# Narrow decay products, scaled rows and reordered last products in a one-core hybrid decoder step

## The chip, the cores and the metric

The kernel runs on one core of one Trainium2 chip. The metric is the device time of one execution in microseconds; the time of a version is the median of its runs.

## What is computed

One layer of a hybrid decoder, for 256 prompt rows and 8 sample rows (264 columns, since activations are held transposed, channels on the partitions), with a model width of 2048. All of it is in fp32. Cut to what matters:

```python
mod = silu(c) @ w_ada + b_ada                      # 6 vectors of 2048 per row
h   = rmsnorm(x) * (1 + sc1) + sh1
z   = h @ w_in                                     # 2048 -> 15376
y_a = spatial gating (LayerNorm, causal 128x128 per group)
y_b = HGRN2 recurrence, 8 heads of 128x128
y_c = GLA recurrence, 4 heads of 128x256
merged = sum_n sigmoid(z_gate_n) * (y_n @ w_branch[n])
x  = x + gt1 * rmsnorm(merged @ w_out)
h2 = rmsnorm(x) * (1 + sc2) + sh2
x  = x + gt2 * rmsnorm(square(relu(h2 @ w_up)) @ w_down)      # 2048 -> 8192 -> 2048
```

The two recurrences are S_t = diag(f_t) S_(t-1) + k_t v_t^T, o_t = S_t^T q_t. Inside a chunk they need, for positions s before t, the products att[t, s] = sum_d q[t, d] k[s, d] exp(b[t, d] - b[s, d]), where b is the running sum of the log decays. The kernel splits them by distance into levels: at level m, two neighbouring blocks of m positions share a reference point, so the decay factors fall apart into one for k and one for q, and one matrix product gives the block.

## The kernel before

**Dense products.** Every weight is read once, in blocks of 512 KB. ScalarE casts each half block to an fp32r high part (`whi`), VectorE subtracts to get the low part (`wlo`); this is `split_half`, with `split` at line 108. TensorE multiplies high by high, high by low and low by high: lines 641, 642, 643. Twenty-four such products are a *granule* (line 631), and the kernel has 578 of them. A granule's weights are split two to three granules ahead of use (`ahead`, line 613): after granule i, the split of granule i+3 is emitted.

**Order.** The order on TensorE and GpSimd is written out by hand in the mixer part, that on TensorE, VectorE and ScalarE around the begin of the MLP (lines 1481 to 1640), and that on TensorE alone in the rest; where it is not, a scheduler decides. After each granule `background` (line 681) runs a piece of other work. It advances a clock `now` by one and pumps two queues of generators, `bg` (the mixers) and `bs` (the states of the samples), at rates set by `RATES` (line 37).

**Mixers.** `mixer_r` (line 1103) runs three times, for two groups of four HGRN2 heads and one of four GLA heads. The levels for distances 16, 8, 4, 2, 1 and the diagonal are put into the list `levels`. `slot` (line 648) takes up to two of them between two granules and multiplies each as 32 products of 32 columns by 32, in the four 32-column quarters of the array (line 661); `copy_predicated` merges the result (line 1136). Levels 32 and 64 each have 8 products with 128 stationary and 64 moving columns (line 1190), of which the parts needed are copied to `att`; they run at a place of their own. After them come the products over distance 128 (line 1214), transposes (line 1221) and the states. `slot` also takes the sample products (line 668) and the `ada` products for `mod` (line 362).

**Begin of the MLP.** The input of the MLP must be the normed rows, transposed. `quad(q)` (line 1543) makes four of the 16 channel tiles. `quad(0)` adds the residual within TensorE. For q > 0, `residual(q)` (line 1536, VectorE) first adds it in place, and `quad` multiplies each 128x128 piece of the rows by `diag(r2)` (line 1560), which scales and transposes in one. `put_quad` (line 1569) modulates, splits and stores. In `begin_up` (line 1588) the quads and residuals stand between the first eight granules: quad 1 after granule 0, residual 2 after granule 1, quad 2 after granule 2, and so on; the tiles of quad q are first read by granule 2q.

**End.** In the last pass of `down` (line 1622) each of eight blocks of 256 channels is gated, and its rows are transposed back (`to_tokens`, line 828, four transposes) after the next granule. After the last block, three of the eight 128x512 output pieces are made on TensorE: identity times residual (line 1666), then diag(r3) times the rows (line 1675). `norms` (line 1445) has the products that give the last norm, `r3`.

Of the kernel before, what the change touches and what calls it, by code (L numbers as in the profile page):

```python
# [15 lines left out]
P = 128  # L16
# [19 lines left out]
CHUNKS = (2, 2, 4, 4, 4)  # L36
RATES = ((1.8, 0.5), (1.6, 0.5), (1.25, 0.5), (1.0, 0.5))
ST_BUFS = 4
# [19 lines left out]
def hybrid_step_kernel(  # L58
# [396 lines left out]
    hh, hl = [], []  # L455
    A1 = const([P, KT, NC], "A1")
# [115 lines left out]
    class Stream:  # L572
# [27 lines left out]

        def split_half(self, i):
# [3 lines left out]
            split(self.raw[i].pop(0), hi, lo)  # L605
            self.parts.setdefault(i, []).append((hi, lo))

        def split(self, i):
# [39 lines left out]
    def slot():  # L648

        lv = [x for x in levels if x[0] + AGE <= now[0]][:2]  # L650
        sv = [x for x in samples if x[0] + AGE <= now[0]]
        del levels[:len(lv)]
        del samples[:len(sv)]
        if lv:
            pl = sm([P, 2, 8, 32])
            for i, (_, lhs, rhs, _) in enumerate(lv):
                for h in range(4):
                    for hf in range(2):
                        for b in range(4):
                            t0 = hf * P + b * 32  # L660
                            T.matmul(pl[32 * b:32 * b + 32, i, 2 * h + hf, :], lhs[:, h, t0:t0 + 32], rhs[:, h, t0:t0 + 32], start=True, stop=True)  # L661
        if sv:
# [6 lines left out]
        if rounds.due():  # L669
            rounds.steps()  # L670
        for i, (_, _, _, put) in enumerate(lv):
            put(pl[:, i])
        if sv:
# [105 lines left out]
    rows = first.rows()  # L779
    stream[0].split_half(0)  # L780
    next(rows)
# [321 lines left out]
    def mixer_r(G):  # L1103
# [30 lines left out]
        def level(li, lhs, rhs):  # L1134
            def put(ps):
                V.copy_predicated(a32, msk[:, li:li + 1, :].to_broadcast([P, 8, 32]), ps)

            levels.append((now[0], lhs, rhs, put))

        level(5, k, q)  # L1140
        for li, m in enumerate(LEVELS):
# [19 lines left out]
            yield  # L1161
        yield lambda: not levels
        for b in range(4):
            r = slice(32 * b, 32 * b + 32)
            S.copy(att[r, :, r], a32[r])
        yield

        for m in (32, 64):
            n = NP // (2 * m)
            e = blk()  # L1170
            ev, cv = v4(e, 2 * m), v4(c, 2 * m)
# [11 lines left out]

            yield READY
            ps = sm([P, 8, 64])
            for h in range(4):
                for hf in range(2):
                    b = e[:, h, P * hf:P * hf + P]
                    rhs = b.rearrange("p (n j) -> p n j", j=2 * m)[:, :, m:2 * m]
                    T.matmul(ps[:, 2 * h + hf, :].rearrange("p (n j) -> p n j", j=m), b, rhs, start=True, stop=True)  # L1190
            yield
            if m == 32:
                S.copy(att[0:32, :, 32:64], ps[0:32, :, 0:32])
                S.copy(att[64:96, :, 96:128], ps[64:96, :, 32:64])
            else:
                S.copy(att[0:64, :, 64:128], ps[0:64])
# [18 lines left out]
        yield  # L1215
        S.copy(attx, ps)
        kt = blk([P, 2, 512])
        for hf in range(2):
# [323 lines left out]

    def quad(q):

# [3 lines left out]
        for i2 in range(2):  # L1548
# [3 lines left out]
            for i in range(2):  # L1552
# [5 lines left out]
                for t in range(2):  # L1558
                    o = pk[:, t * P:(t + 1) * P]
                    T.matmul(o, x1[t][q // 2][:, c0:c0 + P], dg[:, t, :], start=True, stop=q > 0)  # L1560
                    if q == 0:
                        T.matmul(o, og[t][0][:, c0:c0 + P], dg[:, 2 + t, :], start=False, stop=True)
# [17 lines left out]
    quad(0)  # L1580
    residual(1)

    rate[:] = (0.0, 0.0)
# [4 lines left out]
    def begin_up():  # L1588

        accs = [new_acc(), new_acc()]  # L1590
        for k in range(0, KT, 2):
            granule(w_mlp_up[0], 0, 2, 0, 2 * CW, accs, h2H, h2L, k, k == 0, k + 2 == KT)
            if k % 4 == 0 and k + 4 < KT:
                quad(k // 4 + 1)
            elif k + 6 < KT:
                residual(k // 4 + 2)
            elif k + 2 == KT:
                residual(0)
            if k >= 8:
                background()  # L1600
# [18 lines left out]
    y2 = [blk() for _ in range(4)]  # L1619
    yt = None  # L1620

    def down(f, ah, al):
        for m in range(8):
# [9 lines left out]
            if f == NFB - 1:  # L1633
                g = gated(m, dst, G2)
                if m < 7:
                    later.append((now[0], lambda m=m, g=g: put_rows(m, to_tokens(g), yt)))
                else:
                    return g

    zs = begin_up()  # L1640
# [21 lines left out]

    pt = to_tokens(g)
    for i, p in enumerate(by_pe):
        sums_pe[p] = acc[:, i, :] if i < 2 else sm()
        T.matmul(sums_pe[p], ident, piece(x1, *p), start=True, stop=False, skip_group_check=True)
        if i == 1:
            r3 = norms()
    put_rows(7, pt, yt)
# [73 lines left out]
```

## Time and profile before

| | us |
|---|---|
| Median of 3 runs | 1939.91 (1939.54 to 1941.91) |
| The profiled execution | 1938.26 |
| its span, first to last instruction | 1936.5 |
| VectorE busy | 1186.6 (61%) |
| ScalarE busy | 1002.7 (52%) |

The profile is of one execution. Its groups list, per source line, the busy time, the mean duration of one instruction in ns, and the idle time of the engine just before. Matmuls overlap in the records: a row of 0.28 us doesn't mean that the next one starts 0.28 us later, so distances between starts are used below. An fp32 product shows as two records, an fp32 transpose and an fp32r product as one.

### The profile page before, as it was taken

The page shows a single profiled execution, that of the slowest core. Times are in us where ns is not written, and L with a number is a line of the kernel's source. Part 1 is how long each engine was busy: PE and PEld are TensorE (multiplying, and loading weights), DVE is VectorE, ACT ScalarE, POOL GpSimd, SP SyncE. Part 2 cuts the span into 40 slices and gives each one's busy share as a digit, 9 for nine tenths or more (in the row PEclk, how much of TensorE's full clock was granted, in tenths as well). Part 3 has the DMA queues.
Part 4 walks back from the last instruction along what each step waited for, and adds up shares of the span by engine and source line. Part 5 has one row for each costly group of instructions (what it writes and reads, how often), then busy time and mean ns, then how long its engine had stood idle before and what let it go on. Part 6 is the DMA issues. An engine that isn't in the chain of part 4 may idle for free.

```text
span 1936.5 us, 42145 instructions
## 1 busy us (share of the span) xinstructions
PE 1903.5 (98%) x17012; PEld 1813.5 (94%) x17012; DVE 1186.6 (61%) x2092; ACT 1002.7 (52%) x1818; POOL 84.8 (4%) x146
## 2 busy tenths in 40 slices
PE   7999999999999999999999999999999999999998
PEld 5889999999999989899999989999999999999997
DVE  4566667686676784555555666545556555555665
ACT  5434454665855755544444555444444545454544
POOL 1000000001101111100000010000000000000000
PEclk9999999999999999999999999999999999999999
DMA  9897786778778778887777846676665656555552
GB/s 334 318 331 252 232 299 205 227 257 263 230 254 253 228 255 262 288 271 250 255 257 230 302 124 214 221 239 185 184 181 179 185 177 184 180 180 182 180 182 100
DMA packets 339395, 442.05 MB, mean 228 GB/s; under 512 B 14946, under 2 KB 281040, under 8 KB 339200
## 3 DMA queue, kind: packets, MB, share of 16 engines
q1 hardware_dynamic: 329136, 409.62, 65.8%
q0 software_dynamic: 8992, 28.48, 4.5%
q8 instruction: 133, 2.18, 0.4%
q10 hardware_dynamic: 1072, 1.25, 0.2%
q14 instruction: 62, 0.51, 0.1%
HBM read 427.60 MB, written 11.70 MB: 227 GB/s over the span
## 4 chain that ended last, share of the span: by engine, by line
PE 95%; DMA 3%; DVE 1%; ACT 1%; issue 0%; SPq 0%; POOL 0%; DVEq 0%; ACTq 0%
PE mm L641 29%; PE mm L642 28%; PE mm L643 28%; PE ada L362 3%; DMA b<-in_w_ada_dram 2%; PE ada L294 1%; DMA vbc<-vs_d 1%; PE sm L833 1%; PE sm L661 1%; PE sm L1190 1%; PE sm L668 1%; DMA b<-in_x_prompt_dram 0%; PE sm L1560 0%; DMA raw<-in_w_in_dram 0%; DVE wlo L106 0%
## 5 line engine op out<-in xcount | busy, mean ns | idle before, releaser
L641 PE MATMUL mm<-b,whi 128*128 128x264 f32 x4624 | 1325.2, 287 | 2.4 <-ACT b L109 1.6
L643 PE MATMUL mm<-b,wlo 128*128 128x264 f32 x4624 | 1311.9, 284 | 4.1 <-DVE wlo L106 2.6
L642 PE MATMUL mm<-b,whi 128*128 128x264 f32 x4624 | 1313.0, 284 | 1.9 <-issue 1.0
L106 DVE TENSOR_TENSOR wlo<-raw,whi 128x512 fp32r<-128x512 f32 x1136 | 776.7, 689 | 561.8 <-ACT whi L109 557.9
L109 ACT CAST whi<-raw 128x512 fp32r<-128x512 f32 x1136 | 696.1, 618 | 741.7 <-PE mm L642 654.8
L641 PEld LDWEIGHTS mm<-b,whi 128*128 128x128 f32 x4624 | 869.8, 188 | 44.7 <-issue 26.7
L643 PEld LDWEIGHTS mm<-b,wlo 128*128 128x128 f32 x4624 | 869.4, 188 | 6.2 <-DVE wlo L106 3.4
L642 PEld LDWEIGHTS mm<-b,whi 128*128 128x128 f32 x4624 | 869.7, 188 | 1.5 <-DVE b L106 1.2
L103 DVE TENSOR_TENSOR b<-b,mm 128x528 f32<-128x528 f32 (+1 forms) x137 | 95.7, 699 | 41.9 <-PE mm L643 41.7
L1087 DVE SCALAR_TENSOR_TENSOR st<-vbc,b,st 128x128 f32<-128x128 f32 (+1 forms) x96 | 34.2, 390 | 59.6 <-DMA vbc<-vs_d 56.2
L1085 ACT ACTIVATE st<-st,fs 128x128 f32<-128x128 f32 (+1 forms) x96 | 37.2, 431 | 53.9 <-DMA st<-in_state_hgrn_dram 27.2
L362 PE MATMUL ada<-araw,cT 128*32 128x512 f32 x296 | 39.8, 601 | 0.0
L294 PE MATMUL ada<-b,cT 128*32 128x256 f32 (+1 forms) x640 | 35.0, 353 | 3.2 <-DMA b<-in_w_ada_dram 3.0
L100 DVE TENSOR_TENSOR b<-b,b 128x512 f32<-128x512 f32 (+1 forms) x47 | 33.8, 740 | 1.3 <-ACT b L1203 1.1
L294 PEld LDWEIGHTS ada<-b,cT 128*32 128x32 f32 x640 | 17.8, 113 | 15.8 <-DMA b<-in_w_ada_dram 7.6
L1088 POOL DMA_DIRECT2D out_dram<-st x32 | 23.5, 735 | 127.7 <-DVE st L1087 122.9
L362 PE MATMUL ada<-b,cT 128*32 128x512 f32 x216 | 26.2, 593 | 0.0
L106 DVE TENSOR_TENSOR b<-gt,b 128x528 fp32r<-128x528 f32 x32 | 22.7, 708 | 3.2
L106 DVE TENSOR_TENSOR b<-b 128x1024 f32<-128x1024 f32 (+1 forms) x24 | 24.3, 1016 | 0.0
L109 ACT CAST whi<-araw 128x512 fp32r<-128x512 f32 x20 | 12.4, 620 | 21.5 <-PE mm L642 17.2
L100 DVE TENSOR_TENSOR gt<-vt 128x528 f32<-128x528 f32 x32 | 22.5, 702 | 0.9 <-ACT vt L1608 0.9
L1614 ACT ACTIVATE b<-vt 128x528 fp32r<-128x528 f32 x32 | 20.7, 648 | 1.0
(345 smaller groups left out, 839.6 us busy)
## 6 DMA issues: line engine op xcount, KB each, us to landing
raw<-in_w_in_dram SPq DMA_DIRECT2D x231, 512.0 KB, 4.7
raw<-in_w_mlp_up_dram SPq DMA_DIRECT2D x128, 512.0 KB, 3.9
raw<-in_w_mlp_down_dram SPq DMA_DIRECT2D x128, 512.0 KB, 3.6
b<-in_w_ada_dram SPq DMA_DIRECT2D x102, 512.0 KB, 6.4
araw<-in_w_ada_dram SPq DMA_DIRECT2D x74, 512.0 KB, 5.7
raw<-in_w_branch_dram SPq DMA_DIRECT2D x48, 512.0 KB, 4.7
raw<-in_w_out_dram SPq DMA_DIRECT2D x32, 512.0 KB, 3.9
b<-in_w_ada_dram SPq DMA_DIRECT2D x32, 256.0 KB, 5.4
```

The costliest lines, as they stand in the source:

```text
L100: V.tensor_tensor(o, a, b, op=ALU.mult)
L103: V.tensor_tensor(o, a, b, op=ALU.add)
L106: V.tensor_tensor(o, a, b, op=ALU.subtract)
L109: S.copy(hi, src)
L294: T.matmul(acc[32 * j:32 * j + 32, 0:n], cT[:, k, :], w[:, n * j:n * j + n], start=k == 0, stop=k == KT - 1)
L362: T.matmul(self.acc[32 * j:32 * j + 32, :], cT[:, k, :], ws[j // 2][:, j % 2 * 512:j % 2 * 512 + 512], start=k == 0, stop=k == KT - 1)
L641: T.matmul(o, a, xh(k + j), start=first and j == 0, stop=False)
L642: T.matmul(o, a, xl(k + j), start=False, stop=False)
L643: T.matmul(o, b, xh(k + j), start=False, stop=last and j == n - 1)
L1085: S.activation(st[:, i, :], st[:, i, :], AF.Copy, scale=fs[:, h0 + i, b:b + 1])
L1087: V.scalar_tensor_tensor(st[:, i, :], v[:, i, :], k[:, h0 + i, NP + b:NP + b + 1], st[:, i, :], ALU.mult, ALU.add)
L1088: nc.gpsimd.dma_start(G.s_out(b, h0, nh), st)
```

## The change

1. **Levels 32 and 64** go through `levels` and `slot` too, as 16 products of 32 stationary columns each, with 32 and 64 moving columns; only the needed blocks are computed. A level 64 takes a slot alone. The copies to `att` follow in the slot; the copies of the smaller levels move behind the distance-128 products, and those wait three background steps.
2. **`RATES`** of the background goes from 1.6 to 1.8 and from 1.25 to 1.4 in two stages.
3. **MLP input:** for q > 0 ScalarE scales the rows by `r2` into new tiles (`scaled`, two activations of 128x512 per quad, emitted right after the residual), and TensorE transposes these against the identity.
4. **Start:** the first half block's `wlo` is subtracted after the first tile of `h` is split, not before.
5. **End:** rows of two blocks are transposed in one go; the products of the last norm come ahead of the three identity products.

```diff
-RATES = ((1.8, 0.5), (1.6, 0.5), (1.25, 0.5), (1.0, 0.5))
+RATES = ((1.8, 0.5), (1.8, 0.5), (1.4, 0.5), (1.0, 0.5))
...
                 if j == 0:
                     V.tensor_copy(h, p)
                     sub(l, p, h.bitcast(F32))
+                    if w_lo:
+                        w_lo.pop()()
...
+            S.copy(hi, raw)
+            if later:
+                return lambda: sub(lo, raw, hi.bitcast(F32))
+            sub(lo, raw, hi.bitcast(F32))
...
         lv = [x for x in levels if x[0] + AGE <= now[0]][:2]
+        if any(x[3] == 64 for x in lv):
+            lv = lv[:1]
...
+        for _, lhs, rhs, m, _ in lv:
+            if m == 64:
+                pl = sm([P, 8, 64])
+            else:
+                two = two or sm([P, 2, 8, 32])
+                pl = two[:, len(pls)]
+            pls.append(pl)
+            n = max(m, 32)
+            for h in range(4):
+                for hf in range(2):
+                    for b in range(4):
+                        if m >= 32 and b // (n // 32) % 2:
+                            continue
+                        t0 = hf * P + b * 32
+                        q0 = t0 if m < 32 else hf * P + b // (n // 32) * n + n
+                        T.matmul(pl[32 * b:32 * b + 32, 2 * h + hf, :], lhs[:, h, t0:t0 + 32], rhs[:, h, q0:q0 + n], start=True, stop=True)
...
-        yield lambda: not levels
-        for b in range(4):
-            r = slice(32 * b, 32 * b + 32)
-            S.copy(att[r, :, r], a32[r])
-        yield
 
         for m in (32, 64):
             n = NP // (2 * m)
+            yield lambda: len(levels) < 2
...
-            yield READY
-            ps = sm([P, 8, 64])
-            for h in range(4):
-                for hf in range(2):
-                    b = e[:, h, P * hf:P * hf + P]
-                    rhs = b.rearrange("p (n j) -> p n j", j=2 * m)[:, :, m:2 * m]
-                    T.matmul(ps[:, 2 * h + hf, :].rearrange("p (n j) -> p n j", j=m), b, rhs, start=True, stop=True)
...
+            levels.append((now[0], e, e, m, put))
 
         cv = v4(c, P)
+        yield lambda: len(levels) < 2
...
-        yield READY
-        yield READY
+        t0 = now[0]
+        yield lambda: now[0] >= t0 + 3
         attx = blk([P, 4, P])
...
         S.copy(attx, ps)
+        yield lambda: not levels
+        for b in range(4):
+            r = slice(32 * b, 32 * b + 32)
+            S.copy(att[r, :, r], a32[r])
+        yield
...
+    def scaled(q):
+
+        rows = [tmp([P, 4, P], "gt") for _ in range(2)]
+        for t in range(2):
+            S.activation(rows[t].rearrange("p k f -> p (k f)"), x1[t][q // 2][:, q % 2 * 512:q % 2 * 512 + 512], AF.Copy, scale=r2[:, t:t + 1])
+        return rows
...
-                    T.matmul(o, x1[t][q // 2][:, c0:c0 + P], dg[:, t, :], start=True, stop=q > 0)
-                    if q == 0:
+                    if q > 0:
+                        T.transpose(o, rows[t][:, 2 * i2 + i, :], ident)
+                    else:
+                        T.matmul(o, x1[t][0][:, c0:c0 + P], dg[:, t, :], start=True, stop=False)
...
     quad(0)
     residual(1)
+    rows = [scaled(1)]
...
             if k % 4 == 0 and k + 4 < KT:
-                quad(k // 4 + 1)
+                quad(k // 4 + 1, rows.pop())
             elif k + 6 < KT:
                 residual(k // 4 + 2)
+                rows.append(scaled(k // 4 + 2))
...
+    def rows_out(ms):
+        for (m, _), pt in zip(ms, [to_tokens(g) for _, g in ms]):
+            put_rows(m, pt, yt)
...
+                if m % 2 or m == 6:
+                    later.append((now[0], lambda ms=tuple(gs2): rows_out(ms)))
+                    gs2.clear()
...
     pt = to_tokens(g)
+    r3 = norms()
     for i, p in enumerate(by_pe):
         sums_pe[p] = acc[:, i, :] if i < 2 else sm()
         T.matmul(sums_pe[p], ident, piece(x1, *p), start=True, stop=False, skip_group_check=True)
-        if i == 1:
-            r3 = norms()
     put_rows(7, pt, yt)
```

More of the change, by code (lines that the diff above doesn't have):

```diff
@@ L599, in load, with split_half @@
             self.raw[i] = [t[:, 0:n // 2, :], t[:, n // 2:n, :]]
-        def split_half(self, i):
+        def split_half(self, i, later=False):
             n, width = self.items[i][2], self.items[i][4]
@@ L653, in slot @@
         del samples[:len(sv)]
[L654 to L661 removed]
+        pls, two = [], None
+        for _, lhs, rhs, m, _ in lv:
[14 more added lines that the diff above has]
+                        T.matmul(pl[32 * b:32 * b + 32, 2 * h + hf, :], lhs[:, h, t0:t0 + 32], rhs[:, h, q0:q0 + n], start=True, stop=True)
         if sv:
@@ L670, in slot @@
             rounds.steps()
-        for i, (_, _, _, put) in enumerate(lv):
-            put(pl[:, i])
+        for pl, x in zip(pls, lv):
+            x[4](pl)
         if sv:
@@ L779, in hybrid_step_kernel @@
     rows = first.rows()
-    stream[0].split_half(0)
+    w_lo.append(stream[0].split_half(0, True))
     next(rows)
@@ L1136, in put @@
                 V.copy_predicated(a32, msk[:, li:li + 1, :].to_broadcast([P, 8, 32]), ps)
-            levels.append((now[0], lhs, rhs, put))
+            levels.append((now[0], lhs, rhs, 1, put))
         level(5, k, q)
@@ L1541, in residual, with quad @@
             V.scalar_tensor_tensor(x, og[t][q // 2][:, cs], r1[:, t:t + 1], x, ALU.mult, ALU.add)
-    def quad(q):
+    def scaled(q):
[3 more added lines that the diff above has]
+        return rows
+    def quad(q, rows=None):
         hs, ls = (h[q][:, :, NP:NT] for h in (h2h, h2l))
@@ L1634, in down @@
                 g = gated(m, dst, G2)
-                if m < 7:
-                    later.append((now[0], lambda m=m, g=g: put_rows(m, to_tokens(g), yt)))
-                else:
-                    return g
+                gs2.append((m, g))
+                if m == 7:
+                    return g
+                if m % 2 or m == 6:
+                    later.append((now[0], lambda ms=tuple(gs2): rows_out(ms)))
+                    gs2.clear()
     zs = begin_up()
```

20 lines of the change are left out of this document (9 added, 11 removed).

## The prediction, made before the result

> **What bounds the kernel now.** I read the page's busy shares and slices first, then the groups, then the timeline of TensorE (PE) at the places that the change touches, last the other engines there.
>
> ```profile
> span 1936.5 us, 42145 instructions
> PE 1903.5 (98%) x17012; PEld 1813.5 (94%) x17012; DVE 1186.6 (61%) x2092; ACT 1002.7 (52%) x1818; POOL 84.8 (4%) x146
> L641 PE MATMUL mm<-b,whi 128*128 128x264 f32 x4624 | 1325.2, 287 | 2.4 <-ACT b L109 1.6
> ```
>
> PE is busy 98% of the span (columns: busy us, share, instructions; in a group: count, busy, mean ns, idle before). The granules (line 641 and its two like, 13872 products) are untouched. So the change counts by two things: PE time in the products between granules, and waits of PE that it makes or ends. ScalarE (ACT) and VectorE (DVE) matter only where PE comes to wait for them.
>
> ```profile
> 397.06 0.28 PE L643 MATMUL mm<-b,wlo 128*128 128x264 f32 x1
> ...
> 399.97 0.28 PE L643 MATMUL mm<-b,wlo 128*128 128x264 f32 x1
> ```
>
> These starts lie 24 products apart: 2.91 us is a granule, 0.121 us a product. What stands between granules adds to that.
>
> **Part 1, levels 32 and 64 (lines 1184 to 1196).**
>
> ```profile
> 452.43 1.73 PE sm L1190 x16
> 698.61 1.32 PE L661 MATMUL sm<-b 128*32 128x32 f32 x128
> 704.14 0.76 PE L661 MATMUL sm<-b 128*32 128x32 f32 x64
> 875.63 3.57 PE ada L362 x32
> ```
>
> The chain shows one wide block, 8 products or 16 records, at 1.73 us. Six go (two levels, three groups): 10.4 us. A small level is 64 records; the second one in a run costs 1.32 - 0.76 = 0.56. Its records go round the four quarters of the array: 16 rounds of 0.035. The new level 32 has 16 products, so 32 records, in two quarters: again 16 rounds, 0.56 if a quarter sets the pace, 0.28 if each record costs 0.56/64. I take 0.56, since the same quarter must load new weights each round either way. Level 64 streams 64 columns, not 32. Line 362 has 8 rounds of 512 columns in 3.57, 0.87 ns a column, so a round gains 0.028 and the block costs 16 x 0.063 = 1.0; it lies between 0.56 (the columns hide) and 1.73 (no better than the old block). Per group 3.46 - 1.56 = 1.9 us goes, in all 5.7.
>
> The order of instructions on PE also shows 50 runs of such products between granules 109 and 236, where there were 53. A run of its own costs 0.76 - 0.56 = 0.20 beyond its products, and the first granule product behind it comes late by 0.1; runs of transposes cost no such thing (below). Three runs are worth 0 to 0.9; I take 0.6. Part 1: **-6.3 us**, between -3.5 and -8.8.
>
> A rule speaks against this. The Trainium skill, "TensorE: Matmul & The Clock Gate", section "Wait — 56ns, not 53.3ns?", says that starts of matmuls are never closer than about 25 ns, however few columns they have. Taken over the whole array, 32 records would cost at least an estimated 0.8 us and part 1 would come to -5.6. The trace doesn't agree with it across quarters: 64 records in 0.56 us are 9 ns each.
>
> **Part 2, faster background.** It moves the same instructions of DVE and ACT, a few granules earlier, and the third group's states with them.
>
> ```profile
> 395.00:845.00 450.00, 444.68 (x4762) 415.10 (x4761) 302.78 (x574) 276.65 (x570) 65.83 (x99) 1.00 0.81 259
> PE mm L643 <- DVE wlo L106: 2.6, 3, 1.2
> ```
>
> In the mixers' window (columns: length, PE, PEld, DVE, ACT, POOL busy) DVE is busy 67%, ACT 61%: the work has cover. PE waits 2.6 us for a late `wlo` between 500 and 845, three times. New waits for the levels stand in generators; what is held there isn't in an engine's queue. I cost this at 0, from -2.6 (the late `wlo` go) to +2.6 (they double).
>
> **Part 3, the MLP's input.** On PE alone it is a gain.
>
> ```profile
> 1154.61 0.39 PE L1560 MATMUL sm<-gt,b 128*128 128x128 f32 x2
> 1154.83 0.39 PE L1562 MATMUL sm<-gt,b 128*128 128x128 f32 x2
> ...
> 1917.69 0.29 PE L643 MATMUL mm<-b,wlo 128*128 128x264 f32 x1
> 1917.82 0.60 PE L833 MATMUL sm<-cst,gt 128*128 128x128 f32 x4
> 1918.49 0.29 PE L643 MATMUL mm<-b,wlo 128*128 128x264 f32 x1
> ```
>
> An fp32 product takes 0.22 from start to start. Four transposes lengthen three granule steps from 0.36 to 0.80: 0.11 each. Eight per quad, three quads: 3 x 8 x 0.11 = 2.7 us less. But the transposes now wait for ACT, and the order of ACT and DVE is fixed here: on ACT the two `scaled` stand behind the residual and *ahead* of the two casts that the granule emits; on DVE the two `wlo` of those casts stand ahead of quad's `vt` (line 1572).
>
> ```profile
> 1158.00 2.40 PE L1560 MATMUL sm<-gt,b 128*128 128x128 f32 x16
> 1166.07 2.06 PE L1560 MATMUL sm<-gt,b 128*128 128x128 f32 x16
> 1157.11 1.41 DVE L1541 SCALAR_TENSOR_TENSOR b<-b,nr,b 128x512 f32<-128x512 f32 x2
> 1158.43 1.29 DVE L106 TENSOR_TENSOR wlo<-raw,whi 128x512 fp32r<-128x512 f32 x2
> 1159.64 0.54 DVE L1572 TENSOR_SCALAR vt<-sm,A,mod 128x256 f32<-128x256 f32 x1
> 1164.84 1.41 DVE L1541 SCALAR_TENSOR_TENSOR b<-b,nr,b 128x512 f32<-128x512 f32 x2
> 1172.62 1.41 DVE L1541 SCALAR_TENSOR_TENSOR b<-b,nr,b 128x512 f32<-128x512 f32 x2
> 1175.15 0.54 DVE L1572 TENSOR_SCALAR vt<-sm,A,mod 128x256 f32<-128x256 f32 x1
> 1176.97 0.69 DVE L106 TENSOR_TENSOR b<-vt,b 128x512 fp32r<-128x512 f32 x1 [1.28 <-ACT b L109]
> 1156.33 0.41 ACT L109 CAST b<-vt 128x256 fp32r<-128x256 f32 x1
> 1157.33 1.34 ACT L109 CAST whi<-raw 128x512 fp32r<-128x512 f32 x2 [0.60 <-PE mm L642]
> 1162.90 1.14 ACT L109 CAST whi<-raw 128x512 fp32r<-128x512 f32 x2
> L1411 ACT ACTIVATE gt<-b,G 128x256 f32<-128x256 f32 x8 | 4.0, 495 | 0.0
> ```
>
> Residual 1 ends at 1158.52. A `scaled` of 512 elements isn't in the trace: the same kind at 256 takes 0.495 (line 1411), and a cast goes from 0.41 at 256 to 0.62 at 512 (half of 1.14 and the overlap), so 0.70. The second ends at 1159.26. The casts, before at 1157.33, follow: 1159.19 to 1160.33 (1.14 for a pair in sequence). The second `wlo` runs from 1160.37, DVE is free at 1160.98, and line 1572 starts there and not at 1159.64: **1.35 late**. From it to the next residual the rows form a chain of waits between ACT and DVE, 1164.84 - 1159.64 = 5.20 us, which shifts whole. So residual 2 ends 1.35 late, at 1167.60; its rows are scaled by 1168.35; PE, which began quad 2 at 1166.07, waits, does eight transposes in 0.9 and goes on 1.3 late in spite of the shorter work. Each round adds the same delay: residual 3 is 2.7 late, at 1176.7, PE goes on after quad 3 about 2.65 late, and line 1572 is 4.05 late, at 1179.2. The first low part of quad 3 then ends at 1181.7 (1176.97 + 0.69 + 4.05); the granule that needs it could begin at 1181.25, so its second product waits 0.45. From there PE is **3.1 us** late, and nothing behind gives it back, since PE is the bound. Round after round: the chain needs 9.1 us, two granules and eight transposes only 6.7. Bounds: -2.7 (the chain hides) to +4.1 (PE follows the whole delay).
>
> **Part 4, start.**
>
> ```profile
> 25.08 0.69 DVE L106 TENSOR_TENSOR wlo<-raw,whi 128x512 fp32r<-128x512 f32 x1 [4.03 <-ACT whi L109]
> 25.69 0.19 DVE L103 TENSOR_TENSOR mod<-sm,vec 128x36 f32<-128x36 f32 x1
> 25.88 1.72 PE L774 MATMUL mm<-b,cst 128*128 128x512 f32 x2
> ```
>
> The chain to the first tile of `h` starts 0.6 earlier on DVE, but PE is held by its own warming product until about 27.5. **-0.3**, between -0.6 and 0. What goes behind, `wlo`, is needed two products later.
>
> **Part 5, end.** Transposes cost 0.11 each in runs of 4 as of 8, so pairing blocks is 0. The norm's products come forward:
>
> ```profile
> 1923.05 0.43 DVE L103 TENSOR_TENSOR a<-a,vt 128x264 f32<-128x264 f32 x1
> 1923.25 1.88 PE L1666 MATMUL mm<-b,cst 128*128 128x512 f32 x4
> 1924.97 0.50 PE L1449 MATMUL sm<-cst,a 128*128 128x1 f32 x4
> 1927.55 1.98 PE L1675 MATMUL mm<-b,vt 128*128 128x512 f32 x4 [0.89 <-ACT vt L1673]
> ```
>
> Line 1449 can begin once the last square is added, at about 1923.53 and not 1924.97, so `r3` and diag(r3) come 1.44 earlier. But the three identity products now stand behind it: 0.58 for the norm, 3 x 0.86 for them, and line 1675 can begin at 1926.7, not 1927.55. **-0.85**, between -0.5 and -1.4 (all of `r3`'s lead).
>
> **Sum.** -6.3 + 0 + 3.1 - 0.3 - 0.85 = -4.35 us. The profiled execution took 1938.26, its span of 1936.5 and 1.8 around it, so it would take 1933.9; the median of the runs shown is 1939.91, 1.65 above that, and my forecast for a median is **1935.6 us**, with a range of its own from 1932.5 (part 1 at -8.8, the rest slightly better) to 1938.9 (part 1 at -3.5 and a little of part 2).
>
> **Rivals.**
>
> *The scaling hides.* Were the casts that stand behind `scaled` not needed in time, part 3 would be -2.7: 1935.6 - 5.8 = 1929.8. For it speaks that ACT is busy 52% of the span; against it that its free time here stands in front of the casts, where the new work must wait for the residual. 18%.
>
> *The narrow blocks don't do what they say.* If two quarters don't overlap, each record costs its round alone: 32 x 0.035 + 32 x 0.063 = 3.1 against 3.46 per group. Part 1 falls to -1.6: 1940.3. Against it: 128 records in 1.32 us. 10%.
>
> *Slower: DVE blocked by the sample states.* In the third group a DVE instruction at line 1087 waits for a broadcast by DMA, and the `wlo` behind it in the queue wait too.
>
> ```profile
> 803.59 8.78 DMA vbc<-vs_d
> ```
>
> Splits run two to three granules ahead, so it decides once a broadcast holds DVE for longer than about 2 x 2.91 = 5.8 us; this one did, and three such late `wlo` cost PE the 2.6 us above. The third group now runs up to six granules earlier, against the same loads of `w_ada`. Were the other 12 of its 16 steps to wait so, 12 x 0.87 = 10.4 us come on top: 1946.0. 6%.
>
> **How the numbers follow.** About 0.2%, 3.9 us, is what a measurement of this kernel can tell from no change: below 1936.0 is faster, above 1943.8 slower. The forecast has 62%; its median stands just below that bound, so 36 of them are faster and 26 the same. The hiding case adds 18 to faster, the narrow one 10 to same, the blocked one 6 to slower; the remaining 4 (several small things) go half to faster, half to same. Faster 0.56, same 0.38, slower 0.06. The range reaches to the two nearer rivals, 1929.5 to 1940.4, and leaves out some 15%.
>
> **What would show it.** Right (lines of the changed kernel): a run of line 679 with 16 products of 32 columns adds about 0.56 us, one of 64 about 1.0; PE idles ahead of line 1583, waiting for ACT at line 1562, 0.5 to 2 us per quad, and the MLP's second granule block is about 3 us late against the same granule before; line 1707 starts 0.85 earlier against line 851's last four. Wrong: PE doesn't wait at line 1583; new waits for `wlo` between granules 109 and 236; narrow runs as long as the old ones.

## The result, and the profile after

The changed kernel takes 1943.59 us (median of 20 runs, 1939.67 to 1948.89), the kernel before 1940.42 in the same session (20 runs, 1937.40 to 1944.28). The ratio is 1.0017, 95% interval 1.0011 to 1.0024: some 3 us slower, where 4.35 us faster was forecast.

The page of the changed kernel (span, then busy us, share and instructions of each engine):

```profile
span 1937.8 us, 42318 instructions
PE 1898.9 (98%) x17084; PEld 1805.7 (93%) x17084; DVE 1186.2 (61%) x2094; ACT 1006.5 (52%) x1824; POOL 85.4 (4%) x146
```

TensorE is busy 4.6 us less than before (1903.5), and the span is 1.3 longer: the work went, and waiting came. To find where, I compare the first product of the same granule in both timelines of TensorE. First before, granules 109, 237, 322 and 337:

```profile
407.01 0.39 PE L641 MATMUL mm<-b,whi 128*128 128x264 f32 x1
...
879.13 0.39 PE L641 MATMUL mm<-b,whi 128*128 128x264 f32 x1
...
1154.98 0.37 PE L641 MATMUL mm<-b,whi 128*128 128x264 f32 x1
...
1206.88 0.39 PE L641 MATMUL mm<-b,whi 128*128 128x264 f32 x1
```

Then after, the same four:

```profile
406.46 0.39 PE L648 MATMUL mm<-b,whi 128*128 128x264 f32 x1
...
877.56 0.39 PE L648 MATMUL mm<-b,whi 128*128 128x264 f32 x1
...
1153.30 0.37 PE L648 MATMUL mm<-b,whi 128*128 128x264 f32 x1
...
1208.42 0.39 PE L648 MATMUL mm<-b,whi 128*128 128x264 f32 x1
```

| stretch | before, us | after, us | difference | predicted |
|---|---|---|---|---|
| begin to granule 109 | 407.0 | 406.5 | -0.55 | -0.3 |
| mixers, 109 to 237 | 472.1 | 471.1 | **-1.0** | **-6.3** |
| 237 to 322 | 275.8 | 275.7 | -0.1 | 0 |
| begin of the MLP, 322 to 337 | 51.9 | 55.1 | **+3.2** | +3.1 |
| 337 to 577, the last granule | 711.3 | 712.1 | +0.8 | 0 |
| last granule and end | 18.3 | 17.3 | -1.0 | -0.85 |

The differences add to 1.35, that of the spans. The medians lie 3.2 apart because both profiled executions were quick ones, the changed kernel's more so: its 1939.67 is the least of its 20 runs and 3.9 below their median, while the 1938.26 of the kernel before is 2.2 below that kernel's. Three experiments have the very same mixers, and their traces took 473.0, 473.3 and 476.2 us in that stretch (e9, e7, e3), 2 to 5 more than this one. So the forecast was missed in one place, the mixers, and usually by more than the table shows.

**The narrow blocks do what was forecast.** The timeline of TensorE after, a level 32 (32 columns) and, further on, a level 64 in a run of its own:

```profile
714.14 0.66 PE L679 MATMUL sm<-b 128*32 128x32 f32 x29
714.61 0.62 PE L362 MATMUL ada<-araw,cT 128*32 128x512 f32 x1
...
722.52 1.09 PE L679 MATMUL sm<-b 128*32 128x64 f32 x32
723.54 0.39 PE L648 MATMUL mm<-b,whi 128*128 128x264 f32 x1
```

Level 32 takes 0.53 us from its first start to that of the next row of other products (in the rows above, its last three records start among those of line 362). Level 64 takes 1.02 here, 0.1 of it because a granule product follows, and 0.92 in the two other groups. The old blocks took 1.70 to 1.82. The 29 records of the first row start within 0.47 us, 16 ns each. The Trainium skill, "TensorE: Matmul & The Clock Gate", section "Wait — 56ns, not 53.3ns?", has matmuls start at least about 25 ns apart; by this row that doesn't hold across column quarters.

**What ate the gain.** TensorE's waits in the mixers, after, from 395 to 880 us (columns: us in total, times, the longest):

```profile
PE sm L1291 <- ACT b L1282: 4.9, 2, 3.1
PE mm L650 <- DVE wlo L106: 1.7, 3, 1.2
```

The first row is new. Line 1291 holds the transposes of a group's normed rows, line 1282 (ScalarE) the scaling by the norm ahead of them. All of it falls on the third group. TensorE there, after: the last output products of the group, then the transposes.

```profile
763.44 0.59 PE L1271 MATMUL sm<-b,att 128*128 128x256 f32 x2
...
775.94 0.33 PE L1291 MATMUL sm<-cst,b 128*128 128x128 f32 x1 [3.13 <-ACT b L1282]
778.06 2.61 PE L1291 MATMUL sm<-cst,b 128*128 128x128 f32 x11 [1.78 <-ACT b L1282]
```

ScalarE and then VectorE in between (in brackets: idle time just before, and what ended it):

```profile
769.67 0.91 ACT L1103 ACTIVATE st<-st,fs 128x256 f32<-128x256 f32 x2 [3.22 <-DMA st<-in_state_gla_dram]
770.49 0.56 ACT L1273 COPY b<-sm 128x512 f32<-128x512 f32 x1
...
771.62 0.42 ACT L1276 ACTIVATE vt<-b 128x256 f32<-128x256 f32 x1
...
775.38 1.71 ACT L1282 ACTIVATE b<-b,rr 128x256 f32<-128x256 f32 x4 [1.20 <-DVE rr L205]
...
771.07 0.88 DVE L1105 SCALAR_TENSOR_TENSOR st<-vbc,b,st 128x256 f32<-128x256 f32 x2 [2.71 <-DMA vbc<-vs_d]
772.17 0.17 DVE L199 TENSOR_SCALAR sx<-ss 128x8 f32<-128x8 f32 x1 [0.22 <-ACT vt L1276]
```

The output products end at 764.0. ScalarE copies them out of PSUM (line 1273) only at 770.49, directly behind the state scaling of line 1103, ahead of which it stood 3.22 us for the fetch of a sample's state. Only then come the squares (line 1276), the norm (line 199 is its first step) and the scaling of the *third group*, which have nothing to do with the samples. They stand behind the state steps in the queues. VectorE is held in the same way: its state step (line 1105) waits for the broadcast of a sample's values, which took 10.5 us from issue to landing, and line 199 stands behind it. But line 199 waits last for the squares, so it was ScalarE's wait that decided here. TensorE met the transposes at 772.8, three granules after the last output products, as the order says, and stood there.

TensorE and ScalarE at the same place before:

```profile
784.33 0.59 PE L1256 MATMUL sm<-b,att 128*128 128x256 f32 x2
...
797.18 1.47 PE L1276 MATMUL sm<-cst,b 128*128 128x128 f32 x12
...
786.12 0.42 ACT L1261 ACTIVATE vt<-b 128x256 f32<-128x256 f32 x1
...
789.39 0.51 ACT L1085 ACTIVATE st<-st,fs 128x256 f32<-128x256 f32 x1 [1.71 <-DMA st<-in_state_gla_dram]
790.31 0.91 ACT L1267 ACTIVATE b<-b,rr 128x256 f32<-128x256 f32 x2
```

The squares (line 1261) are done 1.7 us after the output products, before the state step (line 1085) begins to wait; after, it is 8.1 us. And the transposes follow after four granules, 12.3 us, where after TensorE got to them in 8.8. Both differences count: the first transposes of the changed kernel could start 11.9 us behind the output products, which the distance of before would just have covered. The distance goes with the rates: it is 8.8 us in e3, which has the new ones, and 11.5 in e4, which has the old. No wait at line 1276 shows in the list of before. The Trainium skill, "Perfetto Trace Analysis", section "Tensor Engine Instruction (MATMUL, LD_WEIGHTS)", says that ScalarE and VectorE take their work strictly in order; these rows agree.

**The clock behind the wait.** In the middle of it TensorE's granted clock falls to half (columns: length; busy us of PE, PEld, DVE, ACT, POOL; granted clock, busy share of the DMA engines, GB/s):

```profile
777.70:781.10 3.40, 3.04 (x14) 2.79 (x15) 2.59 (x5) 3.40 (x9) 0.00 (x0) 0.50 0.58 176
```

That is why 11 transposes took 2.61 us above, and 12 took 1.47 before. TensorE was busy for 3.04 of these 3.40 us, so some 1.5 us went. From granule 109 to 237 TensorE was idle for 5.3 us before, with no such stretch, and for 8.4 after. Without idle time and without what the half clock took, the mixers come to 466.8 us before and 461.1 after: 5.7 less, which is what the prediction had for the narrow products alone.

**The begin of the MLP** went as forecast. The chief one of TensorE's waits from 1155 to 1192 us, after (before has none there):

```profile
PE sm L1583 <- ACT gt L1562: 3.6, 6, 1.1
```

And two turns of ScalarE, after:

```profile
1165.32 1.39 ACT L1562 ACTIVATE gt<-b,rr 128x512 f32<-128x512 f32 x2 [1.58 <-DVE b L1556]
1174.44 1.38 ACT L1562 ACTIVATE gt<-b,rr 128x512 f32<-128x512 f32 x2 [1.58 <-DVE b L1556]
```

One turn per quad takes 9.12 us, the 9.1 of the prediction, and in each ScalarE waits 1.58 for the residual.

**The end**, after: last transposes, norm products, diag(r3) products.

```profile
1925.13 0.66 PE L851 MATMUL sm<-cst,gt 128*128 128x128 f32 x4 [1.43 <-ACT gt L1426]
1926.01 0.58 PE L1464 MATMUL sm<-cst,a 128*128 128x1 f32 x4 [0.22 <-DVE a L103]
1929.33 1.88 PE L1707 MATMUL mm<-b,vt 128*128 128x512 f32 x4
```

From the last transposes to diag(r3) it is 4.20 us; before it was 4.79 (1922.76 to 1927.55).

### The profile page after: what moved, and what is told of

Its sections match the earlier page's. It is cut to its first block, busy times and chain, and to the rows that moved or that the text cites. A ratio compares the mean times of both kernels' runs of the same rounds, so it can differ in the third digit from the quotient of the medians.

```text
span 1937.8 us, 42318 instructions
## 1 busy us (share of the span) xinstructions
PE 1898.9 (98%) x17084; PEld 1805.7 (93%) x17084; DVE 1186.2 (61%) x2094; ACT 1006.5 (52%) x1824; POOL 85.4 (4%) x146
## 3 DMA queue, kind: packets, MB, share of 16 engines
q10 hardware_dynamic: 1072, 1.25, 0.2%
## 4 chain that ended last, share of the span: by engine, by line
PE 90%; DMA 4%; issue 3%; DVE 2%; ACT 1%; POOL 1%; SPq 0%; DVEq 0%; POOLq 0%; ACTq 0%
PE mm L648 28%; PE mm L649 27%; PE mm L650 27%; PE ada L362 3%; DMA b<-in_w_ada_dram 2%; DMA vbc<-vs_d 1%; PE ada L294 1%; PE sm L679 1%; DVE wlo L106 1%; PE sm L851 1%; DMA st<-in_state_hgrn_dram 0%; PE sm L686 0%; DMA b<-in_x_prompt_dram 0%; ACT whi L610 0%; PE sm L1291 0%
```

## The experiments

Each was compared with the kernel before on the same chip. That kernel took 1939.6 to 1940.8 us there, so rows are best compared by their ratios; the medians are of 4 to 20 runs. The other columns are of each profiled execution. *Idle* is the time from granule 109 to 237 in which TensorE has no product; *clock* is half of the time that it was busy at a granted clock of 0.5 there; *rest* is what is left of the stretch without both.

| | median, us | ratio to before, 95% interval | mixers, 109 to 237 | idle | clock | rest | MLP, 322 to 337 |
|---|---|---|---|---|---|---|---|
| before | 1940.4 | 1 | 472.1 | 5.3 | 0 | 466.8 | 51.9 |
| the change | 1943.6 | 1.0017 [1.0011, 1.0024] | 471.1 | 8.4 | 1.5 | 461.1 | 55.1 |
| e1 old rates | 1941.1 | 1.0004 [0.9995, 1.0013] | 469.1 | 5.9 | 1.7 | 461.5 | 55.2 |
| e2 before, new rates | 1957.2 | 1.0087 [1.0073, 1.0100] | 487.4 | 15.3 | 4.9 | 467.2 | 51.9 |
| e3 old MLP input | 1941.5 | 1.0004 [0.9995, 1.0013] | 476.2 | 10.9 | 3.2 | 462.2 | 51.9 |
| e4 old rates, old MLP input | 1936.7 | 0.9977 [0.9968, 0.9986] | 469.1 | 5.6 | 1.7 | 461.8 | 52.0 |
| e5 e4 + distance | 1933.0 | 0.9963 [0.9950, 0.9977] | 466.7 | 5.0 | 0 | 461.7 | 51.8 |
| e6 e4 + states later | 1950.8 | 1.0060 [1.0047, 1.0072] | 475.6 | 14.8 | 1.8 | 459.0 | 51.9 |
| e7 change, rows early | 1944.1 | 1.0025 [1.0014, 1.0035] | 473.3 | 9.3 | 2.9 | 461.1 | 55.1 |
| e8 change + distance | 1939.2 | 1.0002 [0.9993, 1.0011] | 467.5 | 5.1 | 1.7 | 460.8 | 55.1 |
| e9 change, residual ahead | 1940.7 | 0.9997 [0.9987, 1.0006] | 473.0 | 8.7 | 3.4 | 460.9 | 52.0 |
| e10 e8 and e9 | 1937.9 | 0.9984 [0.9975, 0.9994] | 466.4 | 3.9 | 1.7 | 460.9 | 52.0 |
| e11 e10, old rates | 1931.0 | 0.9945 [0.9928, 0.9963] | 463.6 | 2.2 | 0 | 461.4 | 52.0 |
| e12 before, rates, distances | 1939.6 | 0.9990 [0.9979, 1.0000] | 470.2 | 4.1 | 0 | 466.1 | 51.9 |

The rest is 460.8 to 462.2 us in all versions with the narrow blocks but e6, part of whose work moved behind granule 237, and 466.1 to 467.2 in the three without. So what divides the versions in the mixers is idle time and clock.

The stretch from granule 14 to 109, which no version changes, shows the clock too: ten of these traces have a half-clock spell (a stretch at a granted clock of 0.5) of 3.4 us near 110 us and took 330.3 to 330.8 us, the four without it 328.7 to 329.0.

### e1 to e4: which part of the change costs

Two theories stood against each other for the mixers. *Pace*: the new `RATES` bring work to TensorE before the other engines have it ready. *Slots*: the narrow blocks in common runs shift the samples' products against the loads of `w_ada`, whatever the rates. The expectations call them A and B.

e1 takes the new rates back, e2 puts them alone into the kernel before, e3 takes the MLP input back, e4 both.

```diff
 e1, e4
-RATES = ((1.8, 0.5), (1.8, 0.5), (1.4, 0.5), (1.0, 0.5))
+RATES = ((1.8, 0.5), (1.6, 0.5), (1.25, 0.5), (1.0, 0.5))
 e3, e4
-                    if q > 0:
-                        T.transpose(o, rows[t][:, 2 * i2 + i, :], ident)
+                    T.matmul(o, x1[t][q // 2][:, c0:c0 + P], dg[:, t, :], start=True, stop=q > 0)
...
-    rows = [scaled(1)]
...
-                rows.append(scaled(k // 4 + 2))
```

e1, expected:

> The changed kernel with the old RATES (1.6 and 1.25 in the second and third stage). Theory A, pace: the faster background brings the third group's last transposes close behind the steps of the sample states, which hold ACT and DVE for a DMA; PE then waits at the transposes (6.4 us in the profile after). With the old rates this wait goes: about 4.4 us below before (ratio 0.9978) and some 7.5 below the changed kernel; the third group's transposes come 3 to 4 granules behind its norm. Theory B, slots: the narrow blocks in common runs shift the sample products against the loads of w_ada, whatever the rates: time stays within 2 us of the changed kernel, about 1943, with a wait of several us for ACT or DVE somewhere between granules 150 and 230.

e2, expected:

> The kernel before with the new RATES only (1.8 and 1.4). Theory A: slower than before by the waits that the changed kernel has too, 4 to 8 us (ratio 1.002 to 1.004), with PE waiting for ACT or DVE near the end of the third group. Theory B: within 2 us of before.

e3, expected:

> The changed kernel with the MLP input made as before (products with the diagonal, no scaled rows). The prediction's chain: 3.2 us below the changed kernel, about 1940.4 (ratio to before 1.000), and no wait of PE at the quads. Rival: the 3.2 us that PE is late after the quads in the profile after are given back or due to something else: within 1 us of the changed kernel.

e4, expected:

> The changed kernel with the old RATES and the old MLP input: narrow blocks, start and end alone. Theory A with the prediction's chain: -6.1 (narrow blocks), -0.5 (start), -1.0 (end), 7.6 us below before, about 1932.8 (ratio 0.996). Theory B: about 1940, no better than before.

Measured: taking the rates back gains 0.0013 beside the new MLP input (e1) and 0.0027 beside the old one (e3 to e4), 2.5 and 5.2 us; taking the MLP input back gains the same two sizes. Each difference is uncertain by about 0.0013. In the mixers of the traces the rates are worth 2.0 us (the change to e1) and 7.1 (e3 to e4), but the four traces with the changed kernel's mixers differ among themselves by 5.1, so neither size is firm. The MLP stretch is worth 3.2 us, about the forecast's size, each time. e4, which keeps the narrow blocks, the start and the end, is faster than the kernel before by 4.5 us, where theory A had 7.6 and theory B none.

The rates alone cost 16.4 us, far more than in the bundle. In the mixers of the trace it is 15.3: 10.0 more idle time and 4.9 for the clock. Waits of TensorE, e2, 395 to 920 us:

```profile
PE sm L1214 <- DVE b L100: 4.6, 1, 4.6
PE sm L1231 <- ACT b L1234: 4.1, 1, 4.1
PE sm L1276 <- ACT b L1267: 3.1, 2, 1.8
```

Every one of these is a step of a group that TensorE reaches before its input is there. So pace is real. But e4, with the old rates, still waits at the transposes (rows of its waits, 395 to 880 us):

```profile
PE sm L1291 <- ACT b L1293: 1.8, 1, 1.8
PE sm L1291 <- ACT b L1282: 0.9, 1, 0.9
```

So the rates aren't all of it, and neither theory alone holds.

### e5, e8: more distance at the transposes

In both, the last transposes of a group come four background steps after the scaling is issued, not one; e5 is e4 with it, e8 the changed kernel with it.

```diff
-        yield READY
+        t1 = now[0]
+        yield lambda: now[0] >= t1 + 4
         o = [blk() for _ in range(nj)]
```

e5, expected:

> e4 (old rates, old MLP input) with the last transposes of a mixer released four granules after the scaling was issued, not one. Queue theory: in e4 the third group's squares, norm and scaling stand in ACT's and DVE's queues behind sample-state steps that wait for their transfers, and TensorE meets the transposes at a fixed distance; the run of products at granule 215 costs 9.4 us where its products need about 3.8. With seven granules (some 24 us) between the last output product and the transposes the 5.6 us go: 1931.5 us (1930 to 1933.5), against 1936.7 for e4. Rival, the wait moves on: the same transfers then hold up the next work that TensorE needs, 1935.5 to 1937.5. Rival, crowding: the later transposes of the first two groups push the products of the next group together, slower than 1937.5.

e8, expected:

> The changed kernel with the last transposes of a mixer released four granules after the scaling was issued, nothing else. Queue theory: the wait of about 6.4 us at the third group's transposes (the run at granule 208 costs 7.66, in the kernel before 1.23) goes, and the first two groups' lose about 1 more: 1937.5 us (1936 to 1939). Rival, the wait moves on to what stands behind: 1942 to 1944. Rival, it was mostly the pace of the new rates, with its waits spread over the three groups: 1940 to 1942.

Measured: -0.0014 (e4 to e5) and -0.0015 (the change to e8), 2.8 us each; the mixers shorten by 2.4 and 3.6 us in the traces. Of e5's 2.4, 1.7 is the half-clock spell, which is gone. e5 came as expected, with 1.2 us of the wait left. e8 just missed its range: its transposes now stand six granules behind the output products and TensorE still waits 3.9 us. The chain of waits of e8 there:

```profile
806.68 6.92 DMA st<-in_state_gla_dram
...
814.10 0.49 ACT st L1103
...
815.10 0.49 ACT b L1294
815.63 0.66 PE sm L1292 x4
```

The norm is long done (the last scaling ends at 800.9). Now the *copies out of PSUM* of the first transposes (line 1294, ScalarE) stand behind the next state step (line 1103), which waits for its transfer, and the next transposes need that PSUM space. The same cause thus holds up whatever stands behind it: the rival "the wait moves on" is half right.

### e6: the state steps later

```diff
-FETCHED = 3
+FETCHED = 5
```

> e4 with the sample-state steps issued five granules after their fetch instead of three (FETCHED 5); the last transposes keep their four granules behind the last output product. Queue theory: what holds the third group's norm is the state step that stands ahead of it and waits 6 to 8 us for its transfers; issued two granules (some 7 us) later it finds them landed, ACT and DVE don't stand still, and the wait at the transposes goes: 1931 to 1934 us. Rival, the norm's own chain is too long for four granules whatever stands ahead: the wait at the transposes stays, 1936 to 1937.5.

A miss on both sides: 1950.8 us. The chief one of TensorE's waits in e6, 395 to 920 us:

```profile
PE sm L1304 <- ACT os L1117: 19.1, 2, 14.3
```

The wait at the transposes (1291) is indeed gone from the list, as is most of the one for `wlo`; that much speaks for the queue theory. But with each step two granules later the samples' chain becomes too long: at the end of a group TensorE waits for the samples' own norm (line 1304), 14.3 us once. Of the 14.1 us that e6 takes more than e4, 6.5 fall in the mixers and 7.7 behind them, between granules 237 and 322.

### e7, e9: the MLP's rows

e7 issues residual and scaled rows one granule earlier, behind the quad before. e9 issues only the residual earlier, by a whole quad, so that the scaling finds it done.

```diff
 e7
                 quad(k // 4 + 1, rows.pop())
-            elif k + 6 < KT:
-                residual(k // 4 + 2)
-                rows.append(scaled(k // 4 + 2))
+                if k + 8 < KT:
+                    residual(k // 4 + 2)
+                    rows.append(scaled(k // 4 + 2))
 e9
     rows = [scaled(1)]
+    residual(2)
...
             elif k + 6 < KT:
-                residual(k // 4 + 2)
                 rows.append(scaled(k // 4 + 2))
+                if k + 10 < KT:
+                    residual(k // 4 + 3)
```

e7, expected:

> The changed kernel with the residual and the scaled rows of quads 2 and 3 issued one granule earlier, right behind the quad before. Chain theory: quads 2 and 3 wait for a chain that begins at residual and scaling, 1.06+0.34 and 1.07+0.33 us of idle time at their transposes and about 0.5 each at the granule products behind; with the rows a granule ahead two quads lose 0.7 to 1.5 each, quad 1 stays: 1941.3 us (1940.4 to 1942.2), against 1943.6. Rival, the casts and the low parts behind the transposes are what is late, not the rows: 1943 to 1944.3.

e9, expected:

> The changed kernel with the residual of quads 2 and 3 issued one quad earlier, the scaling left in its place, so that the scaling no longer stands behind the residual of the same quad. Ring theory: ACT and DVE run a closed ring for each quad, residual on DVE, scaling on ACT, casts of the weights on ACT, low parts on DVE, transposes, modulation, split; its turn took 9.1 us (1165.32 to 1174.44 between two scalings) against about 8.4 us of products, 1.58 us of it ACT's wait for the residual. Without that wait a turn fits and TensorE's idle 1.06+0.34 and the 0.5 at the granule products of quads 2 and 3 go: ratio to the kernel before lower by 0.0013 to 0.0018 than the change's own, 1940.8 us (1940 to 1941.6). Rival: as with the rows issued early, the wait only moves to another link: 1943 to 1944.5.

Measured: e7 gains nothing, the stretch stays at 55.1 us. Its waits, 1155 to 1192 us:

```profile
PE mm L648 <- ACT b L109: 1.9, 2, 0.9
PE sm L1583 <- ACT gt L1562: 1.5, 4, 0.5
```

The wait left the transposes and came back at the granule products (first row). My chain theory, that the rows come late, fell. What is too long is the closed ring of the two queues: moving a link inside it left its length as it was, 9.13 us from one scaling to the next (1168.53 to 1177.66). e9 takes one wait out of the ring. Its waits in the same window, and its scalings:

```profile
PE mm L649 <- DVE b L106: 1.0, 3, 0.4
PE sm L1583 <- ACT gt L1562: 0.8, 2, 0.5
```

```profile
1160.81 1.39 ACT L1562 ACTIVATE gt<-b,rr 128x512 f32<-128x512 f32 x2 [1.16 <-DVE b L1556]
...
1168.26 1.33 ACT L1562 ACTIVATE gt<-b,rr 128x512 f32<-128x512 f32 x2
...
1176.00 1.33 ACT L1562 ACTIVATE gt<-b,rr 128x512 f32<-128x512 f32 x2
```

The wait for the residual is gone from the second turn on, a turn takes 7.45 and 7.74 us, and 3.1 of the 3.2 us come back.

### e10, e11: both mended; e12: rates with distances

e10 is the changed kernel with the edits of e8 and e9; e11 is that with the old rates of e1. e12 is the kernel before with the new rates and longer distances at three places:

```diff
 e12, against the kernel before
-RATES = ((1.8, 0.5), (1.6, 0.5), (1.25, 0.5), (1.0, 0.5))
+RATES = ((1.8, 0.5), (1.8, 0.5), (1.4, 0.5), (1.0, 0.5))
...
-        yield READY
-        yield READY
+        t0 = now[0]
+        yield lambda: now[0] >= t0 + 3
         attx = blk([P, 4, P])
...
-        yield READY
+        t2 = now[0]
+        yield lambda: now[0] >= t2 + 2
         for h0 in range(0, 4, nh):
...
-        yield READY
+        t1 = now[0]
+        yield lambda: now[0] >= t1 + 4
         o = [blk() for _ in range(nj)]
```

e10, expected:

> The changed kernel with both: last transposes four granules behind the scaling (as in e8, 1939.2 us) and the residual one quad earlier (as in e9). If the two causes are separate places, their gains add: 1936.3 us (1935 to 1937.5). If the ring holds as it stands: 1938.7 to 1939.7.

e11, expected:

> The changed kernel with old rates, the distance of four granules and the residual one quad earlier: e5 (1933.0 us) with the new MLP input in its mended order. Ring theory: three quads cost 1.2 to 1.3 of products each instead of 1.8 to 2.2, about 0.8 of wait is left at quad 1 and 0.5 at the granule products behind it: 1932.2 us (1931 to 1933.3). Rival, the MLP input costs its 3.2 us whatever the order: 1935.5 to 1936.5.

e12, expected:

> The kernel before with the new rates and longer distances: three granules instead of two before the decay products and one more before the outer products (L1214 and L1231 of the kernel before), and four instead of one before the last transposes. With the rates alone it took 1957.2 us, and TensorE stood 4.6 us at L1214, 4.1 at L1231 and 3.1 at L1276. Distance theory: the faster background costs because TensorE meets each step sooner than its in-order queues can deliver; with the distances 1940.5 us (1938 to 1943). Rival, pace: more steps in a granule press on ACT and DVE whatever the distances, 1948 or more.

Measured: the two mends add (1.0017 to 0.9984). e10 still waits 2.5 us at the third group's transposes and ended a little above its range. e11 is the best version of all, faster than the kernel before by 0.55% (0.37 to 0.72%), some 10.7 us, at the lower edge of its range. Its waits in the mixers, 395 to 880 us:

```profile
PE mm L650 <- DVE wlo L106: 1.0, 2, 0.8
PE mm L648 <- ACT whi L610: 0.6, 1, 0.6
PE mm L650 <- issue: 0.4, 1, 0.4
```

No wait at a group's step is left, and the mixers take 463.6 us, 8.6 less than before: 5.4 by the products (the rest column) and 3.1 by less idle time. In e12, 0.0087 above before became 0.0010 below, so with longer distances almost nothing is left of what the rates cost alone. The same distances with the old rates weren't run in the kernel before, so part of this gain may be theirs whatever the rates. e12's largest wait at a group's step, from 395 to 920 us, is this:

```profile
PE sm L1232 <- ACT b L1235: 1.4, 1, 1.4
```

The rates still bring nothing: from e11 to e10 they cost 0.0039 (some 7 us by the medians). The two traces differ by 4.7 us: 2.9 in the mixers, of which 1.7 is e10's half-clock spell, 1.8 from granule 337 to 577, 0.7 at the end, 0.3 between, and 1.0 the other way ahead of granule 109.

## Why the prediction was wrong

1. **Narrow blocks: right.** Forecast 0.56 and 1.0 us, measured 0.53 and 0.92 to 1.02 instead of 1.70 to 1.82. The rest column falls by 5.7 us, the forecast for the products; nothing shows the further 0.6 for fewer runs. The gain is there, but it isn't paid out in the changed kernel.
2. **Faster background, "I cost this at 0": this step failed.** The mixers kept -1.0 of the -6.3 in the profiled run, and were 0.9, 1.2 and 4.1 us *slower* than before in e9, e7 and e3, which have the same mixers. In the profiled run the missing 5.3 us are 3.1 of more idle time, 1.5 of half clock and the 0.6 for fewer runs. The step argued from shares (VectorE 67%, ScalarE 61% busy, "the work has cover") and from the new waits being in generators, not in a queue. Both are true and beside the point. What the rates and the new slots move is the *order* in which instructions enter the two queues, against transfers of 7 to 10 us, and the distance at which TensorE follows. The third group's norm came to stand behind a state step, and TensorE's transposes came a granule closer. The step priced only late `wlo`, up to 2.6 us more. Their waits were 1.7 us in the profiled run, less than the 2.6 of before, but 2.7, 3.0 and 4.6 in e9, e7 and e3. Most of the loss came from a row that the trace of before didn't have, 4.9 us at the transposes, and from the clock behind it, for which the prediction has no term. Its signs watched `wlo` and the narrow runs, so in the profiled run none of those for being wrong showed.
3. **The rival "DVE blocked by the sample states"** had the right place and the right kind of cause, the third group's sample states, but it looked at one engine and one victim. It asked what `wlo` does behind VectorE's broadcast; it didn't ask which *step of the third group* stands behind a state step, on ScalarE too, with a fixed distance to TensorE. Its own victim shows as well, at one place in each of e3, e7 and e9: a `wlo` directly behind a state step (line 1105) for which TensorE stood 2.5 to 2.8 us. Its price, 10.4 us, was too high for the bundle.
4. **MLP input: right,** +3.1 forecast, +3.2 measured, with the turn of 9.1 us. The forecast's picture, a ring whose turn is too long, is confirmed by e9: take 1.58 us of waiting out of the turn, and the cost goes.
5. **Start: no gain is shown.** The first product starts 2.0 earlier (25.04 instead of 27.02), and 0.55 of it is left at granule 109, near the forecast by luck. Most of the 2.0 is clock: from 23.8 to 27.3 us the granted clock was 0.51 before and 1.00 after, and the two groups of products ahead of the first granule took 1.91 and 1.72 us before, 1.04 and 1.02 after. Over all traces granule 14 begins at 77.5 to 78.7 us with the new start and at 77.6 to 78.7 with the old.
6. **End: right in size.** -1.0 from the last granule on, of which 0.6 stands between the last transposes and diag(r3), where 0.85 was forecast. The three traces with the old end took 18.3 to 18.9 us there, those with the new 17.3 to 17.7, but for e8 and e10, 18.4, with a further half-clock spell of 3.4 us. Pairing costs nothing: granules 560 to 576, where it happens, take 52.5 us before and after.

What is shown: that distance at the transposes, the rates and the MLP's ring each cost time, by edits that change one of them; that idle time and half clock make up what the mixers lost, by the table; and, by ScalarE's rows, that in the profiled run the third group's copy and squares stood behind a state step that waited 3.22 us for its fetch. What is only argued: that without this wait the transposes would have been in time, and that the state steps are the cause in the other versions too. e6 and e8 speak for it. That the half clock follows from the waits is argued too: in the mixers every such spell began in a wait or within 1.6 us behind one, but a wait of 2.8 us in e7, for `wlo`, had none behind it, so no run here shows when it comes. A version with one more state buffer, which would let the fetches start earlier, wasn't tried. That the stretch from 337 to 577 took 0.8 us longer isn't explained. It hardly is chance: the four versions with the same mixers (the change, e3, e7, e9) all took 712.1 there, and other versions 710.8 to 712.8, none with a half-clock spell in it.

## What to carry to other kernels

A busy share says nothing about an in-order queue: before moving work there, list what waits for a transfer in it, and which step stands behind that with a fixed distance to the bounding engine. When two in-order engines hand work to each other, add up the turn of the ring and compare it with the bounding engine's turn; moving a link inside doesn't shorten it, removing a wait does. Count more than the length of a wait of TensorE: look at the granted clock behind it. A faster background brought nothing here, where the bounding engine has no free time, and each of its distances must grow with it.

## What was not expected of the hardware

The 256 KB broadcast of the values took 10.5 us in the changed kernel's third group, while the core's DMA engines moved 310 GB/s, and a state fetch 6.9 in e8, at 246 GB/s. The kernel allows three granules for a state, 8.7 us (3 x 2.91) without the products between, and two for the values, 5.8. After waits of TensorE of some us its granted clock was 0.5 for 3.4 us or more, and a product then took 0.22 us from start to start instead of 0.12. And products in 32-column quarters of the array cost 16 ns a record at 32 columns and about 30 at 64 (0.92 to 1.02 us for 32), so for such narrow blocks the columns do count.
